# Neighbourhood attention in a two-layer encoder: the weights times the values of four units in one run

## The chip, the cores and the metric

The kernel runs on one core of a Trainium2 chip. The metric is the device time of one execution in microseconds (us). The core's engines work side by side, each through its own queue in order: TensorE (PE: matrix products and transposes; PEld: loading their stationary operand), VectorE (DVE), ScalarE (ACT), GpSimd (POOL) and SyncE (SP), which issues nearly all transfers (DMAs). Products land in PSUM, a small memory of eight banks; everything else stands in SBUF, with 128 partitions. Engines wait for each other by semaphores, and whatever stands behind a waiting instruction on its engine waits too.

## What is computed

The reference runs two layers on a sequence of 1024 tokens of width 1024, in f32. The first combines differential attention (4 heads) with a gated recurrence. The second, which the change touches, is neighbourhood attention with 16 heads of width 64 over a 16 x 64 grid of tokens: each token sees a clamped window of 8 rows by 16 columns.

```python
logits = jnp.einsum('bhqd,bhikd->bhqik', q_row, k_blk) * scale + bias
logits = jnp.where(col_mask[:, None, :], logits, -jnp.inf)
p = jax.nn.softmax(logits.reshape(B, H, GRID_W, win_r * GRID_W), axis=-1)
out = jnp.einsum('bhqik,bhikd->bhqd', p, v_blk)
y = (out * jax.nn.silu(g)) @ w_out
```

Before each layer stands an RMS norm with a scale and shift that depend on a conditioning vector (the modulation, which loads and sums large weights), behind it a gated residual, and at the end a last RMS norm.

## The kernel before

**Stages.** The kernel works through a start (norm and first projections), the recurrence, differential attention (up to about 500 us), the first output projection with the norm behind it, the neighbourhood layer (about 640 to 1141 us), and the last output projection with the final norm. Large products keep f32 accuracy by splitting each operand into a high and a low part and multiplying three times (`mm3`, lines 194 to 197). The weights come in slabs of 128 x 1024: `load_next` (152) loads one, ScalarE makes the high part (179) and GpSimd the low part (180).

**The neighbourhood layer** goes through 8 pairs of heads and, for each pair, 8 units: 2 halves of the tokens (`hf`) times 4 blocks of 16 columns (`b`). A unit is 128 queries (8 rows x 16 columns) against 12 rows x 24 or 32 columns of keys, for both heads of the pair (`m`). 64 units run through three functions:

- `na_a(u)` asks for the next unit's bias (1137), computes the logits (600, 601; PSUM tile `n`), and then the softmax: VectorE adds the bias and finds the extremum (1162), ScalarE takes the exponential with its sum (1165), VectorE the reciprocal (1168), GpSimd scales (1170). The probabilities stand in `e`, two buffers. The blocks 1 and 2 use the same bias.
- `na_b(u)` transposes them on TensorE (1182; PSUM tile `etr`) and copies them out to `et`, head 0 by VectorE (1188), head 1 by ScalarE (1186).
- `na_c(u)` multiplies them with the values (1206; PSUM tile `no`, one for four units): 3 groups of 4 rows times 2 heads, six products, which the profile shows as 12 instructions. They use 64 of the array's columns each. After each fourth unit the result is gated (1219, or 1213 with `gate1` for the last two pairs).

The values are projected by `v1_job` for two pairs at a time (tile `v`, 256 columns) and written to DRAM (`vd`, 1069); `load_v` (1081) reads them back by blocks, four transfers a block, into `vch` (`vc` in the profile; five buffers).

**Filler.** The projections of the later pairs (`1v`, `1k`, `1q`, `1g`, products `v` and `pp`) are generators in a queue, `Feed`. `feed.pump(ns)` adds a credit and takes steps until it is used up; a step is six products of 512 columns or twelve of 256, rated 1300 ns. `feed.upto(name)` takes all steps up to a job that is needed now. The loop over units pumps 1700 ns three times a unit (800 in the last eight): after the logits of unit u + 1, after the transposes of unit u, and after the products of unit u - 1. `mod_part` (291 to 311) adds the modulation's pieces on VectorE at the end of a unit, as `after_dve` places them.

**Order.** A planner puts the instructions of each engine in order: by their place in the program, but one that it believes not ready lets later ones pass. Buffers of a tag are handed on in turn, and a tile waits until the readers of its buffer's last content are done. The constant `sel` (126 to 129), with which `spread` (350) spreads a norm's factors over the partitions, stands in SBUF from the start to the end.

Of the kernel before, what the change touches and what calls it, by code (L numbers as in the profile page):

```python
# [11 lines left out]
F32 = mybir.dt.float32  # L12
# [84 lines left out]
def kernel(ctx, tc, xT, xTp, small, lamp, adaw, tb, w0, gw, wo0, w1, nab, wo1, out):  # L97
# [25 lines left out]
    V.memset(ones[:], 1.0)  # L123
    eps = const.tile([P, 1], F32, tag="eps", name="eps")
    V.memset(eps[:], EPS)
    sel = const.tile([P, 4, P], F32, tag="sel", name="sel")
    G.memset(sel[:], 1.0)
    G.affine_select(sel[:], sel[:], pattern=[[-32, 4], [0, P]], base=0, channel_multiplier=1,
                    compare_op=ALU.is_equal, fill=0.0)
# [217 lines left out]

    def spread(rr, bc, w=P):
        for j in range(4):
            T.matmul(bc[:, j * w:(j + 1) * w], sel[:, j, :], rr[:, :w], start=True, stop=True)  # L350

    def rstd_bc(ss, n, pool, bc):
        spread(rstd_rows(ss, n, pool), bc)
# [104 lines left out]

    with tc.tile_pool(name="start", bufs=2) as stp, tc.tile_pool(name="ada0", bufs=12) as adp:
        mixp[1] = stp  # L460
        for k in range(KC):
            mix_tile(k, f"xT{k}")
        half = lambda k, hf: mixed[k][:, hf * HF:(hf + 1) * HF]
# [297 lines left out]
    with ExitStack() as l0:  # L761
        ap = l0.enter_context(tc.tile_pool(name="attn", bufs=1))
        vtok = {}

        def values(h):

# [245 lines left out]

    wide(True)
    with tc.tile_pool(name="bound", bufs=2) as bp:
        run, tail = out_layer(0, ato0, xTp, x1d, bp, [4, 5, 6, 7, 0, 1, 2, 3], by_tile,
                              ((0, 0, 0, HF), (KC, 1, 0, HF)))
# [21 lines left out]
    with ExitStack() as l1:  # L1038
# [66 lines left out]
        def late(p):  # L1105
            return p >= NA_PAIRS - 2
# [33 lines left out]

        def na_a(u):
            p, w8 = divmod(u, 8)
# [10 lines left out]
            ps = psp.tile([P, 2, HF], F32, tag="ps", name=f"n{u}")  # L1153
            sums = ap.tile([P, 2], F32, tag="sums", name="sums")
            nm = ap.tile([P, 2], F32, tag="nm", name="nm")
            e = ap.tile([P, 2, 384], F32, tag="e", name="e")
            for m in range(2):
                logits(ps[:, m, :n], ("b", p), m, hf,
                       lambda q: q[:, b * P:(b + 1) * P],
                       lambda k: grid(k[:], 4 * hf, 12, BLK_C0[b], BLK_W[b]))  # L1160
            for m in range(2):
                state["dve"] = V.tensor_tensor_reduce(  # L1162
                    out=e[:, m, :n], in0=ps[:, m, :n], in1=bias["now"][:, m, :n], scale=-1.0,
                    scalar=3.0e38, op0=ALU.add, op1=ALU.min, accum_out=nm[:, m:m + 1]).ins
                A.activation(e[:, m, :n], e[:, m, :n], AF.Exp, scale=-1.0, bias=nm[:, m:m + 1],  # L1165
                             accum_out=sums[:, m:m + 1])
# [7 lines left out]
        def na_b(u, e):  # L1174
# [1 line left out]
            b = u % 4  # L1176
            kn = 4 * BLK_W[b]
            pt = psp.tile([P, 2, HF], F32, tag="ps", name=f"etr{u}")
            et = ap.tile([P, 2, 384], F32, tag="et", name="et", bufs=2)
            for m in range(2):  # L1180
                for j in range(3):
                    T.transpose(pt[:kn, m, j * P:(j + 1) * P], e[:, m, j * kn:(j + 1) * kn],  # L1182
                                ident[:])
            for m in range(2):
                if m:
                    A.activation(et[:kn, m, :], pt[:kn, m, :384], AF.Copy)  # L1186
                else:
                    V.tensor_copy(et[:kn, m, :], pt[:kn, m, :384])  # L1188
            return et

        def na_c(u, et):
            p, w8 = divmod(u, 8)
            hf, b = divmod(w8, 4)
            kn = 4 * BLK_W[b]
            if w8 == 0:
                feed.upto(f"1v{p - p % 2}")
                for n in range(4):
                    load_v(p, n)
                if p == 0:
                    feed.pump(5000.0)  # L1200
            if b == 0:
                ob[0] = ptp.tile([P, HF], F32, tag="pt", name=f"no{u}")
            po = ob[0]
            for j in range(3):
                for m in range(2):
                    T.matmul(po[64 * m:64 * m + 64, b * P:(b + 1) * P],  # L1206
                             vch[p, b][:kn, j + hf, 64 * m:64 * m + 64],
                             et[:kn, m, j * P:(j + 1) * P], start=(j == 0), stop=(j == 2))
            if b == 3:
                if late(p):  # L1210
                    if hf == 0:
                        mix_tile(p, f"o1_{p}")
                    A.activation(mixed[p][:, hf * HF:(hf + 1) * HF], po[:], AF.Copy)
                    written.add((p, hf))
                    gate1(p, hf)
                else:
                    feed.upto(f"1g{p}")
                    m = mixed[p][:, hf * HF:(hf + 1) * HF]
                    V.scalar_tensor_tensor(m, po[:], 0.5, m, ALU.mult, ALU.mult)
            load_ahead(p, w8)  # L1220
# [19 lines left out]
    with tc.tile_pool(name="fin", bufs=2) as fp:  # L1240
# [4 lines left out]
            nc.sync.dma_start(out[k * P:(k + 1) * P, t0:t0 + x.shape[1]], x)  # L1245


        segments = ((0, 0, 0, 512), (0, 1, 0, 256), (0, 1, 256, 512))
        run, tail = out_layer(1, ato1, x1d, None, fp, KORDER1, lambda x: x, segments)
        before = iter(())  # L1250
# [107 lines left out]
```

## Time and profile before

| | |
|---|---|
| median of 3 runs | 1241.4 us (1240.64 to 1245.04) |
| the profiled execution's own time | 1242.87 us |
| its span, first to last instruction | 1240.7 us |
| mean granted TensorE clock | 0.983 |
| TensorE busy (matmul) | 1186.4 us, 96% |
| VectorE, ScalarE, GpSimd busy | 727.5, 552.9, 373.8 us |
| neighbourhood layer, about | 641 to 1141 us |

A matmul's time in the profile runs from its start to its modelled end, and the next starts before that; the pitch from start to start says what it costs. In the timeline a row gives start, length, engine, line, operation, the tile written and those read, shapes, and how many in a row were merged; in brackets the idle time before it and what ended that. In the table by stretches the columns are the busy time of each engine with its number of instructions, then the granted clock, the share of the DMA engines and GB/s. In the table of waits they are the engine and line that waited, what it waited for, the total in us, how often, and the longest. A row of a line gives the shortest, median and longest duration in ns and the first and last start.

### The profile page before, as it was taken

What the parts mean: (1) busy time and instruction counts of PE and PEld (TensorE: products, weight loads), DVE (VectorE), ACT (ScalarE), POOL (GpSimd) and SP (SyncE); (2) the same over time, 40 slices, a digit from 0 to 9 for tenths busy, and PEclk for the clock granted to TensorE, in tenths of its full rate; (3) what the DMA queues carried; (4) which work ended last, traced back from release to release, by engine and by line L of the source; (5) the groups of instructions that cost most, each with busy time, mean ns of one, the idle gap of its engine ahead of it and who ended that gap; (6) DMA issues with size and microseconds to landing.
All of it is one profiled execution on the core that took longest, in us unless ns stands there. A gap on an engine that the chain in (4) does not pass through costs nothing.

```text
span 1240.7 us, 19096 instructions
## 1 busy us (share of the span) xinstructions
PE 1186.4 (96%) x7240; PEld 975.0 (79%) x7240; DVE 727.5 (59%) x1417; ACT 552.9 (45%) x1023; POOL 373.8 (30%) x348
## 2 busy tenths in 40 slices
PE   4989999899999999999999899999999999999997
PEld 3578877778888887777779689888988898877896
DVE  6753966798899889678561443353233324464344
ACT  4337658365656556423352333343243334465211
POOL 2114422133333325433322233233333333324100
PEclk8999999899999999999999899999999999999998
DMA  9511153222132201384433343333332333323312
GB/s 333 184 34 45 41 178 94 97 71 92 30 105 61 83 18 51 107 291 153 144 112 102 126 124 112 109 119 105 103 101 79 102 98 116 85 70 107 144 68 69
DMA packets 81467, 132.24 MB, mean 107 GB/s; under 512 B 7008, under 2 KB 48096, under 8 KB 81376
## 3 DMA queue, kind: packets, MB, share of 16 engines
q1 hardware_dynamic: 81376, 131.03, 33.6%
q8 instruction: 57, 0.93, 0.3%
q14 instruction: 34, 0.28, 0.1%
HBM read 110.03 MB, written 14.68 MB: 101 GB/s over the span
## 4 chain that ended last, share of the span: by engine, by line
PE 78%; DVE 10%; DMA 4%; issue 3%; ACT 2%; SPq 1%; POOL 1%; DVEq 0%; ACTq 0%; POOLq 0%
PE pp L195 15%; PE pp L197 15%; PE pp L196 15%; PE no L1206 4%; PE etr L1182 3%; PE v L195 2%; PE v L196 2%; PE atr L858 2%; PE v L197 2%; PE n L600 2%; PE n L601 2%; PE s L600 2%; PE s L601 2%; DMA vd<-vt 1%; DVE e L828 1%
## 5 line engine op out<-in xcount | busy, mean ns | idle before, releaser
L195 PE MATMUL pp<-ahi,whi 128*128 128x512 f32 (+1 forms) x1040 | 409.1, 394 | 3.3 <-DVE sgb L606 3.3
L197 PE MATMUL pp<-ahi,wlo 128*128 128x512 f32 (+1 forms) x1040 | 400.0, 385 | 0.8 <-POOL wlo L180 0.8
L196 PE MATMUL pp<-alo,whi 128*128 128x512 f32 (+1 forms) x1040 | 398.7, 384 | 0.0
L180 POOL TENSOR_TENSOR wlo<-raw,whi 128x1024 fp32r<-128x1024 f32 x80 | 195.6, 2447 | 332.8 <-ACT whi L179 332.8
L195 PEld LDWEIGHTS pp<-ahi,whi 128*128 128x128 f32 x1040 | 198.2, 191 | 46.3 <-issue 9.4
L197 PEld LDWEIGHTS pp<-ahi,wlo 128*128 128x128 f32 x1040 | 198.1, 190 | 39.7 <-POOL wlo L180 1.2
L196 PEld LDWEIGHTS pp<-alo,whi 128*128 128x128 f32 x1040 | 198.3, 191 | 33.4 <-issue 1.1
L179 ACT ACTIVATE whi<-raw 128x1024 fp32r<-128x1024 f32 x80 | 84.3, 1055 | 132.3 <-PE pp L196 84.1
L1162 DVE CUSTOM_DVE_ANT_0 e<-n,bias 128x288 f32<-128x288 f32 (+1 forms) x128 | 60.2, 505 | 141.2 <-PE n L601 75.3
L1170 POOL TENSOR_SCALAR e<-e,r 128x288 f32<-128x288 f32 (+1 forms) x128 | 70.1, 560 | 193.8 <-DVE r L1168 186.9
L1165 ACT ACTIVATE e<-e,nm 128x288 f32<-128x288 f32 (+1 forms) x128 | 72.8, 570 | 109.6 <-DVE nm L1162 108.9
L832 ACT ACTIVATE e<-e,nm 128x1024 f32<-128x1024 f32 x64 | 73.4, 1148 | 38.3 <-DVE nm L828 37.6
L828 DVE CUSTOM_DVE_ANT_0 e<-s,tb 128x1024 f32<-128x1024 f32 x64 | 76.9, 1217 | 4.0 <-DMA tb<-in_tb_dram 2.1
L196 PE MATMUL v<-wlo,ahi 128*128 128x256 f32 x256 | 72.5, 283 | 2.7 <-POOL wlo L180 2.7
L195 PE MATMUL v<-whi,ahi 128*128 128x256 f32 x256 | 74.7, 292 | 0.0
L197 PE MATMUL v<-whi,alo 128*128 128x256 f32 x256 | 72.3, 282 | 0.0
L295 DVE SCALAR_TENSOR_TENSOR macc<-ada,ctmp,macc 128x512 f32<-128x512 f32 x56 | 47.6, 851 | 28.7 <-DMA ada<-in_adaw_dram 28.3
L849 POOL TENSOR_SCALAR e<-e,r 128x256 f32<-128x256 f32 x32 | 32.9, 1027 | 100.6 <-DVE r L838 42.5
L1186 ACT ACTIVATE et<-etr 96x384 f32<-96x384 f32 (+1 forms) x64 | 31.2, 488 | 68.9 <-DVE et L1188 64.3
L1206 PE MATMUL no<-et,vc 96*64 96x128 f32 (+1 forms) x768 | 60.6, 282 | 0.0
L1206 PEld LDWEIGHTS no<-et,vc 96*64 96x64 f32 (+1 forms) x768 | 42.2, 136 | 21.6 <-issue 19.9
L963 DVE SCALAR_TENSOR_TENSOR xh<-pp,mod,xh 128x512 f32<-128x512 f32 (+1 forms) x40 | 25.6, 642 | 56.8 <-PE pp L197 49.5
(206 smaller groups left out, 2000.0 us busy)
## 6 DMA issues: line engine op xcount, KB each, us to landing
raw<-in_w_dram SPq DMA_DIRECT2D x56, 512.0 KB
ada<-in_adaw_dram SPq DMA_DIRECT2D x96, 256.0 KB
raw<-in_wo_dram SPq DMA_DIRECT2D x24, 512.0 KB
bias<-in_nab_dram SPq DMA_DIRECT2D x32, 288.0 KB
qq<-qq SPq DMA_DIRECT2D x48, 128.0 KB
bias<-in_nab_dram SPq DMA_DIRECT2D x16, 384.0 KB
xT<-in_xT_dram SPq DMA_DIRECT2D x16, 256.0 KB
xh<-in_xTp_dram SPq DMA_DIRECT2D x16, 256.0 KB
```

The costliest lines, as they stand in the source:

```text
L179: A.activation(hi[:], raw[:], AF.Copy)
L180: G.tensor_tensor(lo[:], raw[:], hi[:], ALU.subtract)
L195: T.matmul(ps, lh, rh, start=start, stop=False)
L196: T.matmul(ps, lh, rl, start=False, stop=False)
L197: state["pe"] = T.matmul(ps, ll, rh, start=False, stop=stop).ins
L600: T.matmul(dst, qsel(q[m]), k, start=True, stop=False)
L828: state["dve"] = V.tensor_tensor_reduce(out=e[:], in0=ps[:].rearrange("p a b -> p (a b)"), in1=tbt[h][:, o:o + S], scale=-1.0, scalar=3.0e ...
L832: A.activation(e[:], e[:], AF.Exp, scale=-1.0, bias=nm[:], accum_out=sums[:, m:m + 1])
L1162: state["dve"] = V.tensor_tensor_reduce(out=e[:, m, :n], in0=ps[:, m, :n], in1=bias["now"][:, m, :n], scale=-1.0, scalar=3.0e38, op0=ALU.a ...
L1165: A.activation(e[:, m, :n], e[:, m, :n], AF.Exp, scale=-1.0, bias=nm[:, m:m + 1], accum_out=sums[:, m:m + 1])
L1170: state["pool"] = G.tensor_scalar(e[:, m, :n], e[:, m, :n], r[:, m:m + 1], 0.0, ALU.mult, ALU.add).ins
L1206: T.matmul(po[64 * m:64 * m + 64, b * P:(b + 1) * P], vch[p, b][:kn, j + hf, 64 * m:64 * m + 64], et[:kn, m, j * P:(j + 1) * P], start=(j ...
```

## The change

- `na_c` no longer runs once a unit. It runs once for four units (one half of a pair), with 48 instructions, in the iteration behind the fourth unit's transposes, ahead of the next logits.
- The three pumps of an iteration become one of three times the size, between the logits of unit u + 1 and the transposes of unit u.
- The transposed probabilities go back into `e` instead of a tile `et` of their own; `e` gets five buffers.
- The values of a pair are asked for by `load_ahead` as soon as their job is done, all four blocks together, from the first unit of the pair on; for pair 0 in the iteration of its fourth unit. The additional pump of 5000 ns at pair 0 is gone.
- The bias is loaded by heads, into tiles of half the size with three buffers in all.
- `sel` is no longer a constant for the whole kernel. It is made anew in each of the four stages that use it, in that stage's own pool.

```diff
-    sel = const.tile([P, 4, P], F32, tag="sel", name="sel")
-    G.memset(sel[:], 1.0)
-    G.affine_select(sel[:], sel[:], pattern=[[-32, 4], [0, P]], base=0, channel_multiplier=1,
-                    compare_op=ALU.is_equal, fill=0.0)
...
+    def make_sel(pool):
+
+        sel = state["sel"] = pool.tile([P, 4, P], F32, tag="sel", name="sel", bufs=1)
+        G.memset(sel[:], 1.0)
+        G.affine_select(sel[:], sel[:], pattern=[[-32, 4], [0, P]], base=0,
+                        channel_multiplier=1, compare_op=ALU.is_equal, fill=0.0)
...
-        def load_ahead(p, w8):
+        def load_ahead(p):
 
             if f"1v{p + 1 - (p + 1) % 2}" in feed.done:
-                for b in range(min(4, w8 - 1)):
+                for b in range(4):
                     load_v(p + 1, b)
...
-            bias["next"] = ap.tile([P, 2, 384], F32, tag="bias", name="bias")
-            nc.sync.dma_start(bias["next"][:, :, :n],
-                              nab[2 * p:2 * p + 2, hf, :, BLK_B[b]:BLK_B[b] + n].rearrange(
-                                  "h p n -> p h n"))
+            bias["next"] = []
+            for m in range(2):
+                t = ap.tile([P, 384], F32, tag="bias", name="bias", bufs=3)
+                nc.sync.dma_start(t[:, :n], nab[2 * p + m, hf, :, BLK_B[b]:BLK_B[b] + n])
+                bias["next"].append(t)
...
-            e = ap.tile([P, 2, 384], F32, tag="e", name="e")
+            e = ap.tile([P, 2, 384], F32, tag="e", name="e", bufs=5)
...
-            et = ap.tile([P, 2, 384], F32, tag="et", name="et", bufs=2)
...
                 if m:
-                    A.activation(et[:kn, m, :], pt[:kn, m, :384], AF.Copy)
+                    A.activation(e[:kn, m, :], pt[:kn, m, :384], AF.Copy)
                 else:
-                    V.tensor_copy(et[:kn, m, :], pt[:kn, m, :384])
-            return et
+                    V.tensor_copy(e[:kn, m, :], pt[:kn, m, :384])
+            return e
...
-        def na_c(u, et):
+        def na_c(u, ets):
...
+            hf = w8 // 4
+            po = ptp.tile([P, HF], F32, tag="pt", name=f"no{u}")
+            for b in range(4):
+                kn = 4 * BLK_W[b]
+                for j in range(3):
+                    for m in range(2):
+                        T.matmul(po[64 * m:64 * m + 64, b * P:(b + 1) * P],
+                                 vch[p, b][:kn, j + hf, 64 * m:64 * m + 64],
+                                 ets[b][:kn, m, j * P:(j + 1) * P],
+                                 start=(j == 0), stop=(j == 2))
...
         for u in range(n_units + 1):
+            pump = PUMP1 if u < 56 else 800.0
+            if u and u % 4 == 0:
+                na_c(u - 4, [ets.pop(u - 4 + b) for b in range(4)])
+            if u % 8 == 3:
+
+                p = u // 8
+                feed.upto(f"1v{p - p % 2}")
+                for b in range(4):
+                    load_v(p, b)
+            elif u >= 8:
+                load_ahead(u // 8 - 1)
             if u + 1 < n_units:
                 es[u + 1] = na_a(u + 1)
-            feed.pump(PUMP1 if u < 56 else 800.0)
+            feed.pump(3 * pump)
             if u < n_units:
                 ets[u] = na_b(u, es.pop(u))
-            feed.pump(PUMP1 if u < 56 else 800.0)
-            if u:
-                na_c(u - 1, ets.pop(u - 1))
-            feed.pump(PUMP1 if u < 56 else 800.0)
             after_dve(mod, 1)
```

More of the change, by code (lines that the diff above doesn't have):

```diff
@@ L349, in spread @@
         for j in range(4):
-            T.matmul(bc[:, j * w:(j + 1) * w], sel[:, j, :], rr[:, :w], start=True, stop=True)
+            T.matmul(bc[:, j * w:(j + 1) * w], state["sel"][:, j, :], rr[:, :w], start=True, stop=True)
     def rstd_bc(ss, n, pool, bc):
@@ L460 @@
         mixp[1] = stp
+        make_sel(stp)
         for k in range(KC):
@@ L763 @@
         vtok = {}
+        make_sel(ap)
         def values(h):
@@ L1014 @@
     with tc.tile_pool(name="bound", bufs=2) as bp:
+        make_sel(bp)
         run, tail = out_layer(0, ato0, xTp, x1d, bp, [4, 5, 6, 7, 0, 1, 2, 3], by_tile,
@@ L1162, in na_a @@
                 state["dve"] = V.tensor_tensor_reduce(
-                    out=e[:, m, :n], in0=ps[:, m, :n], in1=bias["now"][:, m, :n], scale=-1.0,
+                    out=e[:, m, :n], in0=ps[:, m, :n], in1=bias["now"][m][:, :n], scale=-1.0,
                     scalar=3.0e38, op0=ALU.add, op1=ALU.min, accum_out=nm[:, m:m + 1]).ins
@@ L1185, in na_b @@
                 if m:
-                    A.activation(et[:kn, m, :], pt[:kn, m, :384], AF.Copy)
+                    A.activation(e[:kn, m, :], pt[:kn, m, :384], AF.Copy)
                 else:
-                    V.tensor_copy(et[:kn, m, :], pt[:kn, m, :384])
-            return et
-        def na_c(u, et):
+                    V.tensor_copy(e[:kn, m, :], pt[:kn, m, :384])
+            return e
+        def na_c(u, ets):
             p, w8 = divmod(u, 8)
[L1193 to L1220, printed above, removed]
@@ L1222 @@
+            if late(p):
+                if hf == 0:
+                    mix_tile(p, f"o1_{p}")
+                A.activation(mixed[p][:, hf * HF:(hf + 1) * HF], po[:], AF.Copy)
+                written.add((p, hf))
+                gate1(p, hf)
+            else:
+                feed.upto(f"1g{p}")
+                m = mixed[p][:, hf * HF:(hf + 1) * HF]
+                V.scalar_tensor_tensor(m, po[:], 0.5, m, ALU.mult, ALU.mult)
         n_units = 8 * NA_PAIRS
@@ L1245, in finish @@
             nc.sync.dma_start(out[k * P:(k + 1) * P, t0:t0 + x.shape[1]], x)
+        make_sel(fp)
         segments = ((0, 0, 0, 512), (0, 1, 0, 256), (0, 1, 256, 512))
```

## The prediction

> **What bounds the kernel now.** I read the page first, then busy time by stretches, then TensorE's waits in the neighbourhood layer (641 to 1141 us), then its timeline.
>
> ```profile
> PE 1186.4 (96%) x7240; PEld 975.0 (79%) x7240; DVE 727.5 (59%) x1417; ACT 552.9 (45%) x1023; POOL 373.8 (30%) x348
> ...
> PE 78%; DVE 10%; DMA 4%; issue 3%; ACT 2%; SPq 1%; POOL 1%; DVEq 0%; ACTq 0%; POOLq 0%
> ...
> L1206 PE MATMUL no<-et,vc 96*64 96x128 f32 (+1 forms) x768 | 60.6, 282 | 0.0
> ```
>
> ```profile
> 690.70:697.00 6.30, 6.30 (x20) 4.91 (x22) 3.01 (x8) 2.93 (x8) 3.38 (x4) 0.55 0.42 143
> ...
> 800.00:900.00 100.00, 100.00 (x691) 85.27 (x690) 38.13 (x102) 36.47 (x87) 31.53 (x38) 1.00 0.38 112
> ```
>
> ```profile
> PE etr L1182 <- ACT et L1186: 4.2, 1, 4.2
> PE etr L1182 <- POOL e L1170: 0.2, 1, 0.2
> ```
>
> From 800 to 900 us TensorE is busy without a gap at a granted clock of 1.00, and the other engines under 40%. In the whole layer it waits for a softmax result 4.4 us. So a longer distance between logits and transposes, one part of the change, removes no wait there: transposes already find their input. What can be won is time in which TensorE counts as busy and does little: the spacing of starts.
>
> ```profile
> 860.11 0.28 PE L197 MATMUL v<-whi,alo 128*128 128x256 f32 x1
> 860.23 0.82 PE L1182 MATMUL etr<-ident,e 128*96 128x128 f32 x6
> 860.80 0.36 PE L195 MATMUL v<-whi,ahi 128*128 128x256 f32 x1
> 861.00 0.28 PE L196 MATMUL v<-wlo,ahi 128*128 128x256 f32 x1
> ...
> 862.18 0.28 PE L197 MATMUL v<-whi,alo 128*128 128x256 f32 x1
> 862.39 0.88 PE L1206 MATMUL no<-et,vc 128*64 128x128 f32 x12
> 863.20 0.39 PE L195 MATMUL v<-whi,ahi 128*128 128x256 f32 x1
> 863.42 0.28 PE L196 MATMUL v<-wlo,ahi 128*128 128x256 f32 x1
> 863.54 0.28 PE L197 MATMUL v<-whi,alo 128*128 128x256 f32 x1
> ```
>
> Filler products start 0.12 us apart (863.42 to 863.54). One unit's twelve products `no` begin 0.21 after the filler before them (0.09 too much), last 0.81 to the next start, and the first filler product behind them takes 0.22 (0.10 too much): 1.00 us a unit. How much of that is switching shows in the last stage, where the planner broke these products into pieces:
>
> ```profile
> 1117.28 0.88 PE L1182 MATMUL etr<-ident,e 128*128 128x128 f32 x6
> 1118.09 0.65 PE L1206 MATMUL no<-et,vc 96*64 96x128 f32 x6
> ...
> 1121.30 0.87 PE L1206 MATMUL no<-et,vc 128*64 128x128 f32 x10
> 1122.09 0.40 PE L600 MATMUL n<-ks,qq 128*128 128x288 f32 x1
> 1122.33 0.30 PE L601 MATMUL n<-ks,ql 128*128 128x288 f32 x1
> 1122.46 0.29 PE L600 MATMUL n<-ks,qq 128*128 128x288 f32 x1
> ...
> 1123.61 0.44 PE L1206 MATMUL no<-et,vc 128*64 128x128 f32 x4
> 1123.98 0.86 PE L1182 MATMUL etr<-ident,e 128*96 128x128 f32 x6
> ...
> 1133.58 0.66 PE L1206 MATMUL no<-et,vc 128*64 128x128 f32 x8
> 1134.17 0.88 PE L1182 MATMUL etr<-ident,e 128*128 128x128 f32 x6
> ```
>
> Four products up to the transposes take 0.37, eight 0.59: four more cost 0.22.
>
> **The change part by part.** *One run of four units.* 48 products follow each other: 0.81 + 9 x 0.22 = 2.79 us. The run now starts right behind transposes: from those to `no` 0.81 (1117.28 to 1118.09), where transposes followed by filler took 0.57 (860.23 to 860.80) plus 0.08 on the next product (0.20 against 0.12): 0.16 more. Behind the run come logits, whose first product takes 0.24 against 0.13 later: 0.11 more. So 3.06 instead of 4.00, 0.94 a run. Units 0 to 55 make 14 such runs: **minus 13.2 us**. The transposes of the other three units stand before logits instead of filler. No row shows that neighbourhood; the nearest are transposes before filler (0.08 lost) and `no` before logits (0.11 lost), so it costs between nothing and 42 x 0.03 = 1.3 us; I take nothing.
>
> [...]
>
> *What the run waits for at its end.* Before, a unit's transposes had filler and another unit's work between them and its products. Now the transposes of the fourth unit stand right before the run, and its twelve products stand at its end: 0.81 + 36 x 0.055 = 2.8 us after the start of the transposes. By then VectorE and then ScalarE must have copied them out.
>
> ```profile
> 861.73 0.49 ACT L1186 ACTIVATE et<-etr 96x384 f32<-96x384 f32 x1 [0.93 <-DVE et L1188]
> ```
>
> ```profile
> 828.93 0.82 PE L1182 MATMUL etr<-ident,e 128*96 128x128 f32 x6
> ```
>
> ```profile
> 833.35 0.49 ACT L1186 ACTIVATE et<-etr 96x384 f32<-96x384 f32 x1 [3.04 <-DVE et L1188]
> ```
>
> Undisturbed, the second copy ends 1.99 us after the transposes' start (860.23 to 862.22), 0.8 before it is needed; at worst, behind filler's own evacuations, 4.91 (828.93 to 833.84), 2.1 late. Of every fourth unit from 7 to 55, 13 in all, five are over 2.8, together 3.3 us late. I take **plus 3**; the ends are 0 and 13 x 2.1 = 27. Queued behind a late run on TensorE is everything: logits, filler, the next transposes. [...]
>
> *Values at the start.* Pair 0 asks for its values when the third projection job has just written them.
>
> ```profile
> 677.33 0.61 SPq L1069 DMA_DIRECT2D vd<-vt  x1
> 678.03 0.40 SPq L152 DMA_DIRECT2D raw<-in_w_dram  x1
> 682.48 2.44 SPq L1081 DMA_DIRECT2D vc<-vd  x4
> 684.96 0.47 SPq L291 DMA_DIRECT2D ada<-in_adaw_dram  x1
> ```
>
> ```profile
> 688.74 0.75 DVE L295 SCALAR_TENSOR_TENSOR macc<-ada,ctmp,macc 128x512 f32<-128x512 f32 x1 [10.41 <-DMA ada<-in_adaw_dram]
> ```
>
> ```profile
> 690.69 1.49 PE L1182 MATMUL etr<-ident,e 128*96 128x128 f32 x6 [4.24 <-ACT et L1186]
> ```
>
> SyncE's queue stands still until the last write of values has landed, then asks for the last four pieces; the modulation load behind them blocks VectorE for 10.41 us, its copies come late, TensorE stands 4.24 us, and at clock 0.55 loses 0.45 x 6.3 = 2.8 more. Before, block 2 and block 3 were wanted only units later. Now the run wants all four blocks at once: by my count of the feed it begins about 677 us (8 us after the last value product, behind four filler steps, logits and transposes), has blocks 0 and 1, and stands from about 678.5 until block 2 is there, asked for at 682.48 and landed some 3 us later: 7 us, then the same slow clock. VectorE's wait falls into the same time. **Plus 3**; minus 7 if both stalls go, plus 8 if the last piece comes at 690.
>
> *The other edits* I take at nothing.
>
> ```profile
> L1081 SPq DMA_DIRECT2D vc<-vd x128: 505/597/686, 653.9 to 1114.2; - x128
> ```
>
> ```profile
> L127 POOL MEMSET sel<- x1: 528/528/528, 0.9 to 0.9; 128x512 f32 x1
> ```
>
> ```profile
> L128 POOL TENSOR_SCALAR_AFFINE_SELECT sel<-sel x1: 635/635/635, 9.2 to 9.2; 128x512 f32<-128x512 f32 x1
> ```
>
> Later pairs ask for their values together: one block has a free buffer, three wait for the run, so 12 loads of 0.6 us, 7.2 us, hold SyncE's queue once a pair. Needed four units (28 us) later, they are hidden; behind them stand weights, bias halves and modulation pieces, which have a unit (7 us) or more. In the last stage a unit takes 3 us, and a bias half behind such a burst can come up to 7 us late: the stage's own breaking up of products costs at least as much now (a unit about 1.2 us of `no` where 0.7 would do), so zero, with 6 either way. Bias by heads, in three buffers: the second head's load waits for the same unit's first reduction, and the whole queue behind it with it; that reduction is one unit before the need, so hidden, except at 3 us a unit, which is in those 6. The selector built three more times is 1.16 us each on a POOL busy 30%: 3.5 if none of it is hidden. Probabilities stored over their own exponentials in five buffers: the oldest is read by the run before the next logits are issued, no new wait. The dropped 5000 ns pump only moves filler: it runs out at unit 55 in both, counted by credits.
>
> **The sum**: 1242.9 (this execution's own time; span 1240.7) - 13.2 + 3 + 3 = 1235.7. It lies 1.5 over the median of the runs, so 1234 by that median. What a measurement here can tell from no change is about 0.5%, 6 us.
>
> **Rivals.** *All of it and more* (0.20): the planner puts filler in front of the first run, and the start's stall of 7.0 goes: 1241.4 - 13.2 + 3 - 7 = 1224. For it: filler is there to be used; against it: the planner kept to the written order in every unit up to 55.
>
> *The run is not one run* (0.22). The planner places what it believes ready; if it believes the fourth unit's copies late, it puts logits or filler inside. Split in two, a run costs 0.34 more, 4.8 in all, and the late copies no longer count: 1241.4 - 13.2 + 4.8 + 3 = 1236; in four pieces nothing is won: 1244. Middle 1240. For it: the pieces of 2, 4 and 10 above; against it: those stood where filler had run out.
>
> *The copies become the wait* (0.16), slower. The filler is now one piece of three pumps, which ends right before the transposes; its evacuations have priority on VectorE and ScalarE. If the second copy ends as late as the worst one above in six runs of ten, 14 x 0.6 x 2.1 = 18 us are lost: 1241.4 - 13.2 + 18 + 3 = 1249. It decides from (13.2 - 3) / (14 x 2.1), a third of the runs, on. For it: 5 of 13 already late; against it: eight of 13 under 2.5.
>
> **How the numbers follow.** The forecast 1234 has 0.42, with its own range 1229 to 1239. Faster by over 0.5% (under 1235.2): 0.27 of the forecast's, all of the first rival and 0.06 of the second, 0.53; slower 0.16, the third; the rest 0.31. The range goes from 1224 to 1249, the ends of the rivals.
>
> **What would show it.** Right: `no` in runs of 48 lasting 2.8 us behind the transposes; TensorE still without gaps after 700 us; the last runs' end some 8 us earlier. Wrong: gaps before a run's last twelve products (the third rival), pieces of 12 or 36 (the second), a gap before 690 us longer than 8 us or none (the start), or gaps in the last eight units with bias loads late.

## The result and the profile after

The changed kernel takes 1234.0 us (median of five runs, 1229.2 to 1234.5) against 1242.1 for the kernel before (five runs, 1240.6 to 1245.0): ratio 0.992, 95% interval 0.990 to 0.994, so about 9 us are gained and the sign is certain. The profiled execution took 1234.1 us, with a span of 1232.4 against 1240.7.

The page of the profile after: busy time by engine, and the group of the weights times values.

```profile
PE 1172.0 (95%) x7240; PEld 979.5 (79%) x7240; DVE 726.1 (59%) x1417; ACT 551.7 (45%) x1023; POOL 379.0 (31%) x354
...
L1207 PE MATMUL no<-e,vc 96*64 96x128 f32 (+1 forms) x768 | 52.4, 280 | 7.8 <-DMA vc<-vd 7.8
```

TensorE issues the same 7240 products and is busy 14.4 us less: the time came out of the spacing of starts, as no wait of that size was there to remove. The products `no` themselves went from 60.6 to 52.4 us, and they now wait 7.8 us for values, which they did not before.

To see where it happened, I cut both profiles at the same events: the first value product of the layer, the transposes of unit 7, those of unit 55, and the end. Busy time by these stretches, before and then after:

```profile
637.98:724.58 86.60, 79.45 (x499) 68.34 (x498) 28.60 (x73) 28.14 (x62) 27.67 (x28) 0.94 0.42 127
724.58:1110.57 385.99, 385.99 (x2554) 325.62 (x2552) 151.50 (x402) 153.22 (x356) 119.67 (x142) 1.00 0.34 101
1110.57:1240.70 130.13, 121.36 (x835) 103.96 (x833) 56.40 (x124) 36.61 (x81) 25.08 (x23) 0.97 0.29 98
```

```profile
640.75:730.71 89.96, 79.47 (x487) 70.41 (x486) 29.96 (x78) 29.03 (x66) 29.32 (x30) 0.92 0.41 125
730.71:1101.00 370.29, 369.95 (x2541) 326.61 (x2540) 147.23 (x395) 150.00 (x350) 118.40 (x139) 1.00 0.35 104
1101.00:1232.40 131.40, 121.03 (x858) 104.30 (x858) 57.76 (x127) 37.41 (x82) 27.82 (x25) 0.98 0.30 102
```

The middle stretch lasts 15.7 us less, the first 3.4 longer, the last 1.3 longer, and the layer began 2.8 us later (640.75 against 637.98); together -8.3. Before reading these as gains and losses, see how much work each stretch holds. The middle one holds 12 filler products of 512 columns fewer than before (2541 against 2554 products; the thirteenth is a transpose at the border). Such products start 0.23 us apart (843.33 to 843.56 in the profile before), so 2.8 of the 15.7 us is work that moved into the first stretch, and **12.9 us is the gain of 12 runs, 1.08 a run**. The first stretch holds these 12 and the products `no` of two units less (4 instead of 6); what makes it longer is time without a busy TensorE, 10.5 us instead of 7.2. The last stretch holds the products of two units more (858 against 835), at about 1 us a unit, and 1.6 us more without a busy TensorE: the two outweigh by 1.3 what the runs gain there.

TensorE's waits in the layer, 637 to 1140 us, after:

```profile
PE no L1207 <- DMA vc<-vd: 7.8, 2, 6.4
...
PE etr L1189 <- POOL e L1178: 0.6, 1, 0.6
PE etr L1189 <- ACT e L1193: 0.3, 1, 0.3
```

The 4.2 us for a copy before the transposes, in the profile before, are gone, and 7.8 for values stand in their place. All of that is at the start: the middle stretch has 0.34 us without a busy TensorE.

One run of the middle stretch, in TensorE's timeline:

```profile
833.16 0.82 PE L1189 MATMUL etr<-ident,e 128*96 128x128 f32 x6
833.91 2.84 PE L1207 MATMUL no<-e,vc 96*64 96x128 f32 x48
836.68 0.44 PE L604 MATMUL n<-ks,qq 128*128 128x384 f32 x1
836.96 0.34 PE L605 MATMUL n<-ks,ql 128*128 128x384 f32 x1
837.14 0.34 PE L604 MATMUL n<-ks,qq 128*128 128x384 f32 x1
```

From the transposes to the run 0.75 us, the run 2.77 (833.91 to 836.68), and the first logit product behind it 0.28, where the next takes 0.18. Ten of the 12 runs of this stretch are whole like this one; in the other two, products of the modulation (`mrow`) stand behind the first six and leave 42. And the copies that the run's end needs, on ScalarE and then on VectorE:

```profile
833.97 0.59 ACT L589 ACTIVATE qq<-pp 64x512 fp32r<-64x512 f32 x1
834.73 0.49 ACT L1193 ACTIVATE e<-etr 96x384 f32<-96x384 f32 x1 [0.17 <-DVE e L1195]
```

```profile
834.08 0.55 DVE L1195 COPY e<-etr 96x384 f32<-96x384 f32 x1 [2.98 <-PE etr L1189]
```

The second copy ends 2.06 us after the transposes began (835.22 against 833.16); the last twelve products need it at about 2.8. The filler's evacuations (`qq`, two of 0.59, the second shown) do stand ahead of it on ScalarE, but they run while VectorE makes the first copy.

### The profile page after: what moved, and what is told of

It reads as the page before. It is cut to its first block, busy times and chain, and to the rows that moved or that the text cites. A ratio compares the mean times of both kernels' runs of the same rounds, so it can differ in the third digit from the quotient of the medians.

```text
span 1232.4 us, 19297 instructions
## 1 busy us (share of the span) xinstructions
PE 1172.0 (95%) x7240; PEld 979.5 (79%) x7240; DVE 726.1 (59%) x1417; ACT 551.7 (45%) x1023; POOL 379.0 (31%) x354
## 4 chain that ended last, share of the span: by engine, by line
PE 82%; DVE 10%; DMA 3%; ACT 2%; issue 1%; POOL 1%; SPq 0%; DVEq 0%; ACTq 0%; POOLq 0%
PE pp L198 16%; PE pp L200 16%; PE pp L199 16%; PE no L1207 4%; PE etr L1189 3%; PE v L199 3%; PE v L200 2%; PE v L198 2%; PE atr L863 2%; PE n L604 2%; PE s L604 2%; PE s L605 2%; PE n L605 2%; PE o L199 1%; PE o L198 1%
## 5 line engine op out<-in xcount | busy, mean ns | idle before, releaser
L198 PE MATMUL pp<-ahi,whi 128*128 128x512 f32 (+1 forms) x1040 | 400.5, 385 | 3.3 <-DVE sgb L610 3.3
L1195 DVE COPY e<-etr 96x384 f32<-96x384 f32 (+1 forms) x64 | 35.4, 554 | 130.4 <-PE etr L1189 129.6
L837 ACT ACTIVATE e<-e,nm 128x1024 f32<-128x1024 f32 x64 | 73.4, 1148 | 38.3 <-DVE nm L833 37.7
L1193 ACT ACTIVATE e<-etr 96x384 f32<-96x384 f32 (+1 forms) x64 | 31.3, 488 | 91.1 <-DVE e L1195 86.7
L1207 PE MATMUL no<-e,vc 96*64 96x128 f32 (+1 forms) x768 | 52.4, 280 | 7.8 <-DMA vc<-vd 7.8
L870 ACT ACTIVATE ath<-atr 128x512 fp32r<-128x512 f32 x64 | 37.9, 596 | 45.8 <-PE atr L863 45.4
```

Source lines behind the costliest of these rows:

```text
L198: T.matmul(ps, lh, rh, start=start, stop=False)
L837: A.activation(e[:], e[:], AF.Exp, scale=-1.0, bias=nm[:], accum_out=sums[:, m:m + 1])
L1207: T.matmul(po[64 * m:64 * m + 64, b * P:(b + 1) * P], vch[p, b][:kn, j + hf, 64 * m:64 * m + 64], ets[b][:kn, m, j * P:(j + 1) * P], start ...
```

## The experiments

Where an interval is given, it is a 95% interval of the ratio to the kernel before. The theory to be tested: each break of a run costs about 0.34 us in switching, and the rest of the change is nothing beside it, but for the stall at the start. The rivals: the gain comes from where the products stand or where the filler stands, from one of the other edits, or a late copy or a late value eats a part of it that can be had.

**The length of a run.** Everything of the change stays, except that the four units of a half are multiplied one by one, or two by two, behind the transposes of as many later units. The values are still asked for ahead, but block by block, as the buffers come free.

```diff
-            if u and u % 4 == 0:
-                na_c(u - 4, [ets.pop(u - 4 + b) for b in range(4)])
+            if u == 4:
+                na_c(0, [ets.pop(b) for b in range(4)])
+            elif u >= 8 and u % n == 0:      # n = 1, or n = 2
+                for v in range(u - 4, u if u == n_units else u - 4 + n, n):
+                    na_c(v, [ets.pop(v + i) for i in range(n)], n)
```

Expected of runs of one unit:

> The changed kernel with the run taken apart: from unit 4 on each unit's products stand alone, four units after its logits, between transposes and the next logits; the first run (units 0 to 3), the filler, the buffers and the loads stay. Theory 'switching' (the gain is the entry into and exit from the 64-column products, paid once in four units): a lone unit between transposes and logits costs 0.17 + 0.81 + 0.06 = 1.04 us by the changed kernel's rows, in a run of four 0.75; 0.29 x 52 units = 15 us more than the changed kernel, about 1249, slower than the kernel before (which has no stall of 8 us at the start). Rival 'placement' (the gain comes from filler in one piece and the longer way from logits to transposes): about 1234, as the changed kernel.

Expected of runs of two:

> The same with runs of two units. Switching: 0.17 + 0.81 + 0.66 + 0.06 = 1.70 us for two units, 0.85 a unit, 0.10 x 52 = 5 us over the changed kernel, about 1239, a third of the way to single units. Placement: 1234.

Runs of one: 1244.5 us, ratio 1.0011 (0.9993 to 1.0029). Runs of two: 1236.9, ratio 0.9953 (0.9935 to 0.9971). So with four, two and one units a run the ratios are 0.9924, 0.9953 and 1.0011: of 1242 us, 3.6 and 10.8 more than with four. The middle stretch of the two kernels, units of one first:

```profile
730.60:1112.60 382.00, 382.00 (x2542) 326.71 (x2541) 147.37 (x393) 152.08 (x350) 118.27 (x139) 1.00 0.34 100
```

```profile
725.00:1100.20 375.20, 374.52 (x2542) 326.81 (x2540) 148.49 (x396) 150.68 (x350) 118.81 (x139) 1.00 0.35 102
```

All three hold the same filler (one product's difference), so the busy times can be set against each other: 382.00, 374.52 and 369.95. From one to two units, 24 of 48 breaks go: 7.5 us, 0.31 each; from two to four, 12 more: 4.6 us, 0.38 each. The rows of the profile before had 0.34 for a break (1.00 for a unit, less 0.66 for its twelve products at 0.055). So going in and out costs about a third of a microsecond here; what that time consists of, no trace shows. With one unit a run nothing is gained over the kernel before as a whole, although its products stand where the change puts them, behind transposes and ahead of logits. Its middle stretch is 382.0 us, where the kernel before has 383.2 for the same filler (385.99 less 2.8): the place is worth at most 1.2 of the 12.9 us. The expected 15 us for runs of one were too much: 0.25 us a unit in the middle stretch instead of 0.29, and nothing in the last stretch (131.1 us, against 131.4 for the change). Runs of two came out 3.6 us over the change where 5 were expected, a third of the way, as expected. A run of two units and its neighbours, in TensorE's timeline:

```profile
874.74 0.82 PE L1189 MATMUL etr<-ident,e 128*128 128x128 f32 x6
875.49 1.53 PE L1209 MATMUL no<-e,vc 128*64 128x128 f32 x24
876.95 0.40 PE L604 MATMUL n<-ks,qq 128*128 128x288 f32 x1
```

Its edge is that of the run of four, 0.75 from the transposes; the 24 products take 1.46 where 48 took 2.77, so a second 24 costs 1.31 and the entry and exit 0.15 inside the run alone.

**Where the filler stands.** The one piece of three pumps is cut again: one pump ahead of the transposes, two behind them. The run then begins behind filler, not behind the transposes that it waits for.

```diff
-            feed.pump(3 * pump)
+            feed.pump(pump)
             if u < n_units:
                 ets[u] = na_b(u, es.pop(u))
+            feed.pump(2 * pump)
```

> The changed kernel with runs of four, but the filler divided again: a third between logits and transposes, two thirds behind the transposes, so that a run stands between filler and logits and the copies of its fourth unit have two thirds of the filler as cover. Switching: entry from filler 0.09 instead of 0.17 from transposes, 14 x 0.08 = 1 us less, 1233 to 1235. Placement: the gain goes back to the kernel before's order, 1240 or more.

1231.6 us, ratio 0.9924 (0.9898 to 0.9949): the same as the change, so the place of the filler isn't what pays either. Its middle stretch:

```profile
723.00:1097.60 374.60, 374.60 (x2560) 329.64 (x2559) 152.04 (x397) 153.42 (x354) 120.76 (x142) 1.00 0.36 105
```

It holds 18 filler products more than the change has there, 4.1 us, which leaves 370.5 against 370.3. What one neighbour gains the next one pays: with filler behind the transposes the first filler product takes 0.31 us (from 819.63 on), where a later one takes 0.23, and the first logit product takes 0.13 (from 823.82 on), like the next.

This kernel also shows where late copies come from. Its transposes stand as in the kernel before, one pump behind the logits, and those of the unit that was latest there (second copy 4.91 us after their start) begin here at 825.73. VectorE's timeline behind them:

```profile
825.30 2.57 DVE L298 SCALAR_TENSOR_TENSOR macc<-ada,ctmp,macc 128x512 f32<-128x512 f32 x1
...
829.50 0.55 DVE L1195 COPY e<-etr 96x384 f32<-96x384 f32 x1
```

A piece of the modulation, two evacuations of filler and the reciprocal stand ahead of the first copy, and the second ends at 830.64: 4.91 again. Of units 7 to 55, 15 are over 2.8 in this kernel and 11 in the one before, the fourth units 19, 31, 35 and 47 in both. In the change, whose transposes stand three pumps behind the logits, three are (3.96, 2.88 and 2.93), none of them a fourth one. Here the late copies cost nothing, as two pumps follow them; what they would cost right before a run, this kernel doesn't show.

**The youngest copies first.** The run multiplies the fourth unit first, whose copies are the youngest.

```diff
-            for b in range(4):
+            for b in (3, 0, 1, 2):
                 kn = 4 * BLK_W[b]
```

> The changed kernel with the fourth unit's twelve products at the front of each run instead of its end, so that nothing covers their copies. Theory 'cover' (the copies end 2.06 us after the transposes' start, and 24 products ahead of them are what hides that): the first product waits for VectorE's copy, about 0.7 us, the next logits then go between (the instruction order shows one product, logits, the rest) and cover ScalarE's, an additional switch costs 0.34: 1.0 us x 15 runs, 1246 to 1250. Rival: the copies are early enough wherever the products stand: 1232 to 1236.

1244.9 us, ratio 1.0018 (1.0005 to 1.0030), 12 us over the change by the ratios and just under the expected 1246 to 1250: the size was nearly right, the way to it was not. TensorE's timeline at the same run:

```profile
832.47 0.82 PE L1189 MATMUL etr<-ident,e 128*96 128x128 f32 x6
...
834.18 0.43 PE L1207 MATMUL no<-e,vc 96*64 96x128 f32 x2
834.54 0.50 PE L199 MATMUL pp<-alo,whi 128*128 128x512 f32 x1
834.98 2.84 PE L1207 MATMUL no<-e,vc 96*64 96x128 f32 x46
```

TensorE does not wait. The planner takes the run for not ready and lets logits and single filler products pass, and all 12 runs of the middle stretch break into 2 and 46. That costs 6.2 us in the middle stretch (376.5 against 370.3), 0.5 a run. The rest is in the last eight units, where no filler is left to pass. TensorE's waits there, 1100 to 1148 us:

```profile
PE etr L1189 <- POOL e L1178: 5.3, 3, 3.3
PE etr L1189 <- ACT e L1193: 2.0, 2, 1.8
```

In the change these were 0.6 and 0.3. So here a late copy cost switching as long as there was filler, and waiting only where there was none.

**The other edits alone.** The kernel before, with the bias by heads and `sel` made four times, and nothing else of the change.

```diff
+    def make_sel(pool):      # called in each of the four stages
...
-            bias["next"] = ap.tile([P, 2, 384], F32, tag="bias", name="bias")
+            bias["next"] = []
+            for m in range(2):
+                t = ap.tile([P, 384], F32, tag="bias", name="bias", bufs=3)
```

> The kernel before with two of the small edits alone: the selector made anew in four stages, and the bias by heads in three buffers. Theory 'nothing': both are hidden, 1242, ratio within 0.4% of 1, and the layer's first value product starts near 638 us. Rival 'early stages': the changed kernel's profile came to that product 2.8 us later than the one of before, and that is the selector: about 1245.

1242.6 us, ratio 1.0010 (0.9994 to 1.0026): nothing, and its first value product starts at 638.8 us, as expected. What the two edits are for, space in SBUF as it seems, no run here shows.

**The start.** First what happened there. TensorE's timeline in the change (the table of waits has both gaps), and then SyncE's queue:

```profile
673.30 0.28 PE L200 MATMUL v<-whi,alo 128*128 128x256 f32 x1
...
683.05 0.88 PE L1207 MATMUL no<-e,vc 128*64 128x128 f32 x12 [1.39 <-DMA vc<-vd]
690.32 2.14 PE L1207 MATMUL no<-e,vc 128*64 128x128 f32 x16 [6.39 <-DMA vc<-vd]
692.39 0.80 PE L198 MATMUL pp<-ahi,whi 128*128 128x512 f32 x1
```

```profile
677.96 3.36 SPq L1087 DMA_DIRECT2D vc<-vd  x3
...
681.94 0.61 SPq L1075 DMA_DIRECT2D vd<-vt  x1
...
687.35 2.45 SPq L1087 DMA_DIRECT2D vc<-vd  x4
```

The last value product started at 673.30 and its result was copied out by 675.7, but the write to DRAM goes out at 681.94, because reads of earlier values stand ahead of it in the queue and wait until the writes that they need have landed (six such waits, 12.9 us together, from 655 to 695). The last four reads then wait from 684.0 to 687.35 for that write. First edit: the values of pair 0 are asked for an iteration earlier, so that their job is done earlier too.

```diff
-            if u % 8 == 3:
+            if u == 2 or u % 8 == 3:
```

> The changed kernel with the values of pair 0 asked for one unit earlier (all steps of the first values job are taken in iteration 2, and the loads follow them). Theory 'start' (the 7.8 us gap before 690 us and the slow clock behind it are the wait of the first run for the last values, some 17 us behind their last product): the run begins about 13 us instead of 7 us after that product, the gap shrinks to 0 to 2.5 us: 7 to 10 us less than the changed kernel, 1224 to 1227. Rival: the modulation load queued behind the value loads on SyncE holds VectorE instead, as in the kernel before, and a gap of about 4 us with its slow clock stays: 1230 to 1234.

1228.6 us, ratio 0.9881 (0.9854 to 0.9908), about 5 us better than the change, between the theory and its rival. TensorE's waits in the layer, and what VectorE did:

```profile
PE no L1207 <- DVE e L1195: 4.9, 1, 4.9
...
PE no L1207 <- DMA vc<-vd: 0.8, 1, 0.8
```

```profile
688.71 0.75 DVE L298 SCALAR_TENSOR_TENSOR macc<-ada,ctmp,macc 128x512 f32<-128x512 f32 x1 [7.57 <-DMA ada<-in_adaw_dram]
...
689.45 0.53 DVE L1195 COPY e<-etr 96x384 f32<-96x384 f32 x1
```

The values come nearly in time (0.8 us late); now the run waits for a copy, as the rival said, which VectorE has behind a piece of the modulation, and that piece waited 7.57 us for its load. SyncE's queue says why:

```profile
683.86 0.47 SPq L294 DMA_DIRECT2D ada<-in_adaw_dram  x1
```

The load was issued at 683.86, right behind the last four reads of values. It is the stall of the kernel before (10.41 us for the same kind of piece), a little shorter. Second edit: in addition, no piece of the modulation is placed behind the first five units; these pieces run later (56 in all, as before).

```diff
-            after_dve(mod, 1)
+            if u > 4:
+                after_dve(mod, 1)
```

> The kernel with pair 0's values a unit earlier, and beside it the pieces of the modulation start only in iteration 5. Theory: the gap of 4.9 us before 690 us is VectorE blocked by a modulation piece whose load stands behind the value loads on SyncE; without it the run waits at most for the last values, 0 to 2.5 us, and the slow clock behind the gap goes as well: 4 to 7 us less, 1221 to 1224. Rival: the values themselves are as late, the gap stays within 1 us of 4.9, no gain: 1227 to 1229.

1221.25 us, ratio 0.9828 (0.9815 to 0.9841): 7 us less, the upper end of the theory, and 20 us under the kernel before. TensorE's two longest waits in the layer, and its timeline at the first run:

```profile
PE v L199 <- POOL wlo L183: 2.8, 1, 2.8
PE n L604 <- DVE nm L1170: 1.5, 1, 1.5
```

```profile
680.86 3.25 PE L1207 MATMUL no<-e,vc 96*64 96x128 f32 x48
```

Both stalls are gone, and with them the slow clock behind them: the stretch from the first value product to the transposes of unit 7 takes 78.8 us at clock 0.98 against 90.0 at 0.92.

**The tail.** In the last eight units the planner breaks the products `no` into pieces, as no filler is left. Besides the second edit, the filler is spread to reach into them.

```diff
-            pump = PUMP1 if u < 56 else 800.0
+            pump = PUMP1 if u < 48 else 1000.0
```

> The same again, with pumps of 1000 ns from unit 48 on instead of 1700 up to unit 55 and 800 after: filler is left for the last eight units, whose runs the planner then breaks up only in the last half. Theory 'tail': pieces cost entries and exits and leave gaps (9.1 us for the last 96 instructions of `no` in the changed kernel's last stage, where two runs take 5.5): 3 to 6 us less than without it. Rival: the single products of the output layer fill those gaps anyway, and what stands there now is missing before: within 1.5 us.

1220.9 us, ratio 0.9823 (0.9810 to 0.9836), which is the same as without it, as the rival had it. Sixty products moved from the middle stretch to the last; the one takes 357.2 us instead of 370.5, the other 143.8 instead of 132.7, and the layer began 2.2 us later in this execution. The end stands at 1219.1 against 1219.2. So filler in the tail is worth 2.2 us at most, and the medians show 0.4. The rival's account, that the products of the output layer fill those gaps anyway, fits; no run shows it by itself.

## Why the prediction was right, and where it was not

The predicted 1234 is the measured median. But two of its terms, by 1.9 and by 3 us, made it too slow, and a later beginning of the layer, which was chance as far as the other kernels show, made up for a part of that.

- **One run of four units, minus 13.2**: right in mechanism, and slightly small. Predicted 0.94 a run, measured 1.08 over 12 runs, which makes 15.1 for 14. Its pieces: from transposes to the run 0.75 (0.81 forecast), the run 2.77 (2.79), the first logit product behind it 0.28 where a later one takes 0.18, 0.10 too much (0.11 forecast). So the step that was mis-sized is the way in, by 0.06. What is still missing to 1.08 is taken up below. Counted by breaks alone, three fewer for four units at 0.34 each, the rows before give an estimate of 14.3 for 14 runs: nearer than my 13.2, and the runs of one, two and four units, at 0.31 and 0.38 a break, bear it out. That the three other units' transposes ahead of logits cost nothing held: from the transposes to the first logit product are 0.57 us (842.95 to 843.53), and that takes 0.08 more than a later one (0.26, 0.18), as with filler behind them. One reading of mine was wrong without a consequence: of the 4.4 us that I called a wait for a softmax result, 4.2 are a wait for a copy of transposes (line 1186).
- **Late copies, plus 3**: this step failed. I took the five late ones of 13 from the profile before (by its rows they are 3.1 us late together, not 3.3) and moved them to the new order. After, the second copy of the fourth unit ends 2.06 to 2.69 us behind the start of the transposes, in all 13, always under 2.8: zero. What makes a copy late is the place of the transposes: behind one pump they meet the modulation's piece and the filler's evacuations on VectorE, behind three pumps they don't, as the kernel with the filler in thirds shows. That the change moves the transposes two pumps later stood in the diff, and the step left it out; the evacuations that the third rival feared do meet the copies, but on ScalarE, which is second in line anyway. Besides, a late copy is paid in another form: in the kernel that takes the youngest copies first the planner breaks the run, 0.5 us, and TensorE does not wait.
- **Values at the start, plus 3**: right in place, cause and size. Gaps of 1.39 and 6.39 us stand in place of one of 4.24; the time without a busy TensorE in the stretch grew by 3.3. The gap's beginning was forecast for 678.5 and came at 681.7, of which 2.8 is the later beginning of the layer. That the run has blocks 0 and 1 was not quite so: the third part of block 1 made the first, short gap. The other end, "minus 7 if both stalls go", is the second edit of the start: without the 3 for copies it gives 1241.4 - 13.2 - 7 = 1221.2, and 1221.25 was measured; with the 15.1 that the runs gain it would be 2 us less, so the tenth is luck here too.
- **The other edits at nothing**: right. The selector and the bias have their own run (1.0010). The loads of values in bursts, the five buffers of `e` and the dropped pump have none; with 0.34 us without a busy TensorE in the middle stretch and the last stretch as it was, nothing is left for them.
- **The sum**: 1242.9 - 15.1 for the runs + 3.4 for the start + 2.8 for the later beginning of the layer = 1234.0, and the profiled execution took 1234.1; by spans the same sum gives 1231.8, and 1232.4 was measured, so it closes to half a microsecond. The 2.8 belongs to that execution: the seven other kernels with the same code up to there began between 636.5 (runs of two) and 640.0 (runs of one). The forecast also took off 1.5 for the distance of the profiled execution before from its median; the one after stands on its median. How the executions without a profile share these out is not recorded. That the forecast fits to a tenth is luck, that it fits within a few us is not.

The rivals: *All of it and more* was right that the start's stall can go, but not by itself: filler did not step in front of the first run. *The run is not one run* fell (no run shows the 0.34 in its sum by itself; it is an estimate from rows, and the runs of one, two and four units gave 0.31 and 0.38): ten of the 12 runs of the middle stretch are whole, 48 products in 2.77. Two are broken once, but by products of the modulation and not for late copies, and the stretch gained more than forecast all the same. *The copies become the wait* fell for the reason above; a loss of about its size came only where the youngest copies are taken first (12 us over the change), and there more by switching and by the last stage than by waits at the runs.

On the clock: behind the gap of 6.39 us and the sixteen products that follow it the first filler product is 0.80 us long, where 0.39 is usual, and so it was behind the 4.9 of the first edit at the start (a first logit product of 0.69 us, where 0.44 is usual). The plus 3 for late copies counted a wait of 2 us at a run as itself alone. Nothing here shows that, and the profile before had a wait behind which more came: at 640.99 us TensorE has waited 2.74 us, and from 641.77 the clock is 0.50 for 3.4 us. The last section has the rows. It cost the forecast nothing, as no run of the change in the middle stretch waits for its copies.

A run's own pitches give a gain of 1.03 (4.00 less 2.77 for the run, 0.10 more from the transposes to it and 0.10 more on the logits behind it), and the stretch gives 1.08. The rest, 0.6 us over the 12 runs, is not accounted for. What the third of a microsecond consists of stays open: no run here takes it apart.

## What to carry to other kernels

Where TensorE is busy without gaps, count how often it changes between products of 64 and of 128 columns of the array: here each visit cost 0.31 to 0.38 us (runs of one, two and four units), about as much with filler ahead of it as with transposes (middle stretch 370.5 and 370.3 us), and putting four visits into one was worth 0.9% (runs of one unit against runs of four) with no wait removed. Look for the stall of such a change at the stage's start, where all that the longer run needs is wanted at once: a write to DRAM and its read-back share one in-order queue with loads that nobody needs yet (a write with its data ready at 675.7 was issued at 681.94), and asking earlier and holding the unneeded ones back (three lines here) was worth 12 us more by the ratios, where the change itself was worth 9. Lateness read from one profile belongs to what stood ahead on the engine at that place; when a change moves the place, read again what will stand there.

## What the runs showed that I had not expected

**Behind waits of 2.7 us and less TensorE's clock fell to half, and behind the same wait it did so in one profile and not in another.** In the profiles of before, after and seven of the eight experiments TensorE is seen to wait 2.7 or 2.8 us at the layer's start for the low part of a weight. TensorE's timeline in the kernel before and in the one with runs of two:

```profile
640.99 0.39 PE L196 MATMUL v<-wlo,ahi 128*128 128x256 f32 x1 [2.74 <-POOL wlo L180]
```

```profile
639.57 0.39 PE L199 MATMUL v<-wlo,ahi 128*128 128x256 f32 x1 [2.75 <-POOL wlo L183]
```

And the stretches of 3.41 us around them, in the same order; behind the busy times, the number after POOL's is the granted clock:

```profile
638.36:641.77 3.41, 0.78 (x6) 0.78 (x7) 2.73 (x4) 1.16 (x2) 2.58 (x2) 1.00 0.62 181
641.77:645.19 3.42, 3.42 (x18) 3.42 (x17) 0.84 (x4) 1.86 (x4) 1.10 (x1) 0.50 0.97 289
```

```profile
634.55:637.96 3.41, 2.27 (x11) 1.65 (x9) 1.01 (x2) 3.33 (x6) 3.17 (x2) 1.00 0.74 221
637.96:641.38 3.42, 1.81 (x14) 1.81 (x15) 1.75 (x3) 0.16 (x1) 1.56 (x1) 1.00 0.85 243
641.38:644.79 3.41, 3.41 (x29) 3.41 (x28) 1.82 (x8) 2.72 (x7) 1.70 (x1) 1.00 0.71 203
```

In the traces of the kernel before and the changed one the granted clock is either 1.00 or 0.50, and up to 1200 us its changes stand whole multiples of 3.41 us apart. So each of the two can be divided into steps of 3.41 us, counted on from a change of its clock. In the kernel before, 2.63 us of the wait fall into one step, and the next is at 0.50. With runs of two (laid from a change of that trace's clock in the same way) the border of two steps cuts the wait into 1.14 and 1.61, and the clock stays at 1.00. Counted over the two traces, in the steps from 100 to 1200 us whose clock is 1.00: of ten with 0.8 to 1.64 us without a busy TensorE, none is followed by a step at 0.50; of ten with 1.83 or more, all are; of those with less than 0.8, none. Why the clock falls, and whether it would do the same elsewhere, these counts don't show.

The kernel with the copies late does it in its last stage, with several waits in one step:

```profile
1138.43 1.11 PE L1189 MATMUL etr<-ident,e 128*128 128x128 f32 x6 [0.56 <-POOL e L1178]
1141.01 1.50 PE L1189 MATMUL etr<-ident,e 128*96 128x128 f32 x6 [1.46 <-POOL e L1178]
```

```profile
1127.40:1134.23 6.83, 6.83 (x53) 6.05 (x53) 1.36 (x7) 2.39 (x6) 1.15 (x2) 0.50 0.02 3
...
1137.65:1141.06 3.41, 1.37 (x8) 0.68 (x8) 1.43 (x6) 2.13 (x6) 1.76 (x4) 1.00 0.01 4
1141.06:1144.47 3.41, 3.41 (x12) 2.44 (x12) 0.55 (x1) 0.49 (x1) 3.41 (x3) 0.50 0.00 0
```

Waits of 0.56 and 1.46 us, which fall into one stretch of 3.41 us with 1.37 of busy TensorE, are followed by 3.4 us at half the clock, and one of 3.27, which ends at 1125.80, by 6.8. Half of 10.2 us is 5.1 us lost at most (an estimate), beside 7.3 us of waits where the change has 1.8; the stretch from the transposes of unit 55 to the end is 8.3 us longer (139.7 against 131.4). So here short waits close to each other cost more than themselves.

In the change, read-backs of values held SyncE's queue until the write before them had landed: the issue of three took 3.36 us, and the last four stood 3.3 before they went out, so that a write whose data were copied out by 675.7 was issued at 681.94. The cost behind the products of 64 columns didn't vanish when their neighbour changed: logits and filler alike lose 0.10 on the first product (0.28 against 0.18 at 836.68 after, 0.22 against 0.12 at 863.20 before). Behind transposes the first product takes 0.08 longer, but starts only 0.03 behind the last of them, where transposes start 0.11 apart, and so six of them cost 0.65 us in all, with logits behind them (842.95 after) as with filler (860.23 before). And a run whose operands are late is not waited for while the planner has other work; it is broken, at 0.5 us, where waiting for the second copy would have taken about 1.3 (2.06 behind the start of the transposes, less 0.75; an estimate from the change's rows).
